# Turning the FFN's inner activations by DMA transfers of 16-bit halves in place of TensorE transposes

## The chip, the cores and the metric

The kernel runs on one core of a Trainium2 chip, as one launch. The time is device time in microseconds for one whole execution. A core has five engines with an instruction queue each: PE (TensorE: matrix products; its loads of the stationary operand are listed apart as PEld), DVE (VectorE), ACT (ScalarE), POOL (GpSimd) and SP (SyncE, which here only issues transfers). Each works through its own queue in order and waits for the others by semaphores. Transfers run on 16 DMA engines.

## The reference

One step of a one-layer backbone on 128 context and 256 latent tokens of width 2048, in float32: adaLN modulation, a mixing sub-layer (gated linear attention and a Fourier branch), and a dense SwiGLU FFN of inner width 5632. What the change touches is the FFN and the last modulation vector, `ga2`:

```python
mod = jax.nn.silu(cond) @ lw['w_ada'] + lw['b_ada']
sh1, sc1, ga1, sh2, sc2, ga2 = [m[:, None, :] for m in jnp.split(mod, N_MOD, axis=-1)]
...
h = rmsnorm(x, lw['norm_pre_ffn']) * (1.0 + sc2) + sh2
ff = (jax.nn.silu(h @ lw['w_ffn_gate']) * (h @ lw['w_ffn_up'])) @ lw['w_ffn_down']
x = x + ga2 * rmsnorm(ff, lw['norm_post_ffn'])
```

All 384 tokens go through the FFN together, as three token tiles of 128.

## The kernel before

**Numbers.** Every float32 operand of a product is split into a high part (a cast on ACT, `whi` for weights) and a low part (a subtraction on DVE, `wlo`). A product is three matmuls: high x high, low activation x high weight, high activation x low weight.

**Chunks and units.** The inner width is cut into 11 chunks of 512 (c = 0 to 10). The first runs with activations stationary the other way round and needs no turn. From c = 1 on, the table `steps` gives the order. A chunk is a row of units, each of which takes one weight tile of 128 x 1024: A0 to A3, B0 to B3, then four times C, E, D, then four times F, G, H, D. The units A, B, C, E, F, G, H make gate and up products of chunk c by a scheme that saves block products, so that some of their weight tiles are sums or differences of others, made on DVE (L1651, L1674, L1675, L1677). The D units are the down projection of chunk c - 1: D0 to D3 stand with C and E, D4 to D7 with F, G and H. On PE, A, B, C and G are 12 matmuls of 512 columns each, E, F and H six, D 18.

**Ten banks** of a chunk's products are evicted into six scratch tiles `ep` of 128 x 512 float32, called `s1`, `sq`, `s5`, `g0`, `g1`, `e2` (ep0 to ep5). At the end of the chunk `g0`, `g1` and `s5` hold the inner activations of the three token tiles, tokens on the partitions. The down projection wants them with the inner width on the partitions, so each tile is turned: in B0, B1 and B2 of the next chunk `turn_hid` issues four PE transposes of 128 x 128 into one PSUM tile `ptr` (L1812), ACT casts it to `hid_hi` and DVE subtracts to get `hid_lo` (L1814). That is done for c = 2 to 10; the chunk that comes last is turned once more, at its own place, outside of the units.

**Order.** PE, ACT, DVE and POOL run in the order in which the code is written. `grab2` is called at the start of each unit: it takes a ready weight pair, runs the list `now` on ACT, starts loads, and splits the weight tile for the unit three further on (one ACT cast, up to three entries of the list `pend`, the DVE sums, then the DVE subtraction). There are four `whi` buffers. SP's order isn't written out: a scheduler puts its transfers into one queue. Weight tiles of A and B are loaded ahead into eight resident slots; those of C, G and D go through two buffers `raw`.

**The last modulation** (`ada_last`) is a generator that is advanced by `step(ada)`. It has four quarters of 16 steps; each step loads a tile of `w_ada` of 256 KB into one of two buffers (L1704) and does two multiply-adds on DVE (L1707, L1709). A quarter ends with 16 small matmuls on PE into `pr` (L1718), an ACT copy to `adev` (L1723), a PE transpose to `ptm` (L1728) and small DVE work. These two closing parts wait, by giving up steps, while the down projection's banks are live (`d_live`). A step is taken at a rate of 0.85 per call. Whatever is left is run in one go behind unit D3 of chunk index 9.

Of the kernel before, what the change touches and what calls it, by code (L numbers as in the profile page):

```python
# [11 lines left out]
F32 = mybir.dt.float32  # L12
F32R = mybir.dt.float32r
U32 = mybir.dt.uint32
AF = mybir.ActivationFunctionType
ALU = mybir.AluOpType
PSUM = bass.MemoryType.PSUM
# [3 lines left out]
P = 128  # L21
# [13 lines left out]
FC = 4  # L35
NFC = FT // FC
G = 1024
# [70 lines left out]
def tile_step(ctx: ExitStack, tc: tile.TileContext, a, o):  # L108
    nc = tc.nc
    PE, ACT, DVE, POOL, SP = nc.tensor, nc.scalar, nc.vector, nc.gpsimd, nc.sync  # L110
# [199 lines left out]
    def take():  # L310
        return ready.pop(0)

    def grab():
        w = take()
        push()
        return w

    def step(side):
        if side is not None:
            next(side, None)  # L320
# [75 lines left out]
    def rsqrt(dst, src, scale):  # L396
        ACT.activation(dst, src, AF.Sqrt, bias=eps_t[:, 0:1], scale=scale)
        DVE.reciprocal(dst, dst)
# [10 lines left out]
    psm = ctx.enter_context(tc.tile_pool(name="psm", bufs=3, space=PSUM))  # L409
    pss = ctx.enter_context(tc.tile_pool(name="pss", bufs=5, space=PSUM))  # L410
    with ExitStack() as s:
# [94 lines left out]
        def xprod(u, kb, w, bank=px):  # L506
            def mm():
                for j, (x_, w_) in enumerate(passes(w)):
                    PE.matmul(bank, w_[:, u * P : (u + 1) * P], hT[x_][:, kb, :], start=j == 0, stop=j == 2)

            return mm, lambda dst=None: flush(xacc[u], kb == 0, dst, bank)
# [9 lines left out]

        ACT.activation(spad[:, :, 0:2], cond, AF.Silu)
        ACT.activation(tmp1, eps_t, AF.Sqrt)
        qs = [pa.tile([P, T], F32, name=f"qsA{n}") for n in range(2)]
        for k in range(KT):
            sq = qs[k] if k < 2 else scr[:, 4 + k % 4, :]
            ACT.activation(sq, xn(k), AF.Square)
            if k >= 2:
# [22 lines left out]
        for kb in range(KT):  # L551
# [59 lines left out]
            for lo, hi, c in segs:  # L611
# [4 lines left out]
                if kb == 0:  # L616
                    ACT.activation(
                        hT[0][:, kb, lo:hi], xr[:, lo:hi], AF.Identity,
                        bias=mods[:, 0, kb, c : c + 1], scale=mods[:, 1, kb, c : c + 1],
# [30 lines left out]
        for t in range(3):  # L650
            vprod(KT - 1, prev[0], range(3), (t,))
            if t < XU:
                mm, fl = xprod(t, KT - 1, prev[1])
# [99 lines left out]
    with ExitStack() as s:  # L753
# [11 lines left out]
        for c in range(2):  # L765
# [3 lines left out]
            SP.dma_start(raw3[1 + c][96:98, 0:512], src[32:33].to_broadcast([2, 512]))  # L769
        mask = pg.tile([P, 2, CH], U32, name="mask")  # L770
        ss = pg.tile([P, 3, 4], F32, name="ss")
# [7 lines left out]
        def gla():  # L779
# [10 lines left out]
            for h in range(NH):  # L790
# [26 lines left out]
                for n in range(2):  # L817
                    ACT.activation(lap[n], z[n], AF.Abs)
                ACT.activation(la, la, AF.Exp, scale=-1.0)
# [145 lines left out]
        for c in range(2):  # L965

            dst = a2.rearrange("p (h d j) -> p d h j", d=2, j=P)[:, c]
# [129 lines left out]
    with ExitStack() as s:  # L1097
# [166 lines left out]
        for b, i in mix_order:  # L1264
# [18 lines left out]
            else:  # L1283
# [10 lines left out]
                p = psm.tile([P, T], F32, tag="mm", name="pmm")  # L1294
                w = grab()
# [18 lines left out]
    with ExitStack() as s:  # L1314
# [49 lines left out]
        for i in range(KT):  # L1364
            p = psm.tile([P, T], F32, tag="mm", name="pmm")
            for g in range(2):
                n = 2 * i + g - 2 * KT
                if n < -6:
                    w = grab()
                else:  # L1370

                    w = take()
# [178 lines left out]
        def unit(t, n):  # L1551

            return psums[n // 2][:, 3 * (n % 2) + t, :]

        hid = hid_of()
# [8 lines left out]
        pend, now = [], []  # L1564

        def left_sums():

            raw = [psums[n // 3][:, 2 * (n % 3) : 2 * (n % 3) + 2, :].rearrange("p a (b c) -> p (a b) c", c=P) for n in range(4)]
            f = lambda x: x.bitcast(F32)
            h11, h12, h21, h22 = ([f(x) for x in Hx(t, k)] for t, k in ((1, 0), (1, 8), (2, 0), (2, 8)))  # L1570
            r1, r2, r4, r3 = raw
            add, sub = DVE.tensor_add, DVE.tensor_sub

            def parts(dst, src):
                return [lambda: ACT.copy(dst[0], src), lambda: sub(dst[1], src, f(dst[0]))]

            ops = [lambda: add(r1, h21[1], h22[1]), lambda: add(r1, r1, h21[0]), lambda: add(r1, r1, h22[0])]
            ops += [lambda: sub(r2, r1, h11[1]), lambda: sub(r2, r2, h11[0])]
            ops += parts(S1, r1)
            ops += [lambda: sub(r4, h12[1], r2), lambda: add(r4, r4, h12[0])]  # L1580
            ops += parts(S2, r2)
            ops += [lambda: sub(r3, h11[1], h21[1]), lambda: add(r3, r3, h11[0]), lambda: sub(r3, r3, h21[0])]
            ops += parts(S4, r4)
            return ops, parts(S3, r3)

        pend, s3_parts = left_sums()
# [100 lines left out]
        def grab2(kept=2):  # L1687
            w = take()
            while now:
                now.pop(0)()  # L1690
            load_more(kept)
            split_next()
            return w
# [52 lines left out]
        for u in range(HEAD):  # L1746
            kind, c, j = ffn_order[u]
            dst_of[kind](hp[u], c, j)
        n = 0
        for kind, c, j in ffn_order[HEAD:]:  # L1750
            p = psm.tile([P, T], F32, tag="mm", name="pmm")
# [30 lines left out]
        s1, sq, s5, g0, g1, e2 = ep  # L1782

        def evict(c, kind):
# [19 lines left out]
            elif kind == "H":  # L1804
                pend.extend([lambda: add(e2, e2, B["p4"]), lambda: mul(s5, s5, e2)])

        def turn_hid(dst, t, pool, tag):

            pt = pool.tile([P, FC, P], F32, tag=tag, name="ptr")
            src = (g0, g1, s5)[t]  # L1810
            for j in range(FC):
                PE.transpose(pt[:, j, :], src[:, j * P : (j + 1) * P], ident)  # L1812
            hi, lo = (x[:, :, t * P : (t + 1) * P] for x in dst)
            pend.extend([lambda: ACT.copy(hi, pt), lambda: DVE.tensor_sub(lo, pt, hi.bitcast(F32))])  # L1814
# [10 lines left out]
        def out(u, p, c):  # L1825
            if c == 0:
                ACT.copy(u, p)
            else:
                DVE.tensor_add(u, u, p)
            d_live[0] -= 1  # L1830
# [4 lines left out]
        for kind, c, i in steps[:-4]:  # L1835
            last_c = c == NFC - 1 and kind == "D"
            if last_c and hid_last is not None and x1b is None:
                while pend:
                    pend.pop(0)()
                x1b = actp.tile([P, KT, T], F32, tag="A_hi", name="x1b")  # L1840
                for q in range(4):
                    SP.dma_start(x1b[:, 4 * q : 4 * q + 4, :], x1_d[:, 4 * q : 4 * q + 4, :])
                ACT.activation(tmp1, eps_t, AF.Sqrt)
            if kind == "D":
                w = grab2()
                n, kh = i // 2, i % 2
                if kh == 0:
                    while pend:
                        pend.pop(0)()

                    pool, tag = (pss, "side") if done % 2 or (c, n) == (NFC - 2, 3) else (psm, "mm")
                    pd_tiles = [pool.tile([P, 512], F32, tag=tag, name="pdn") for _ in range(3)]
                    d_live[0] = 3
                h = hid_last if last_c else hid
                todo = [
                    (pd_tiles[t], [[x[:, 2 * kh + m, t * P : (t + 1) * P] for m in range(2)] for x in h], mov_d, kh == 0, kh == 1)
                    for t in range(3)
                ]
                products(w, todo)
                if kh == 1:  # L1860
                    if not last_c:
                        for t in range(3):
                            pend.append(lambda u=unit(t, n), p=pd_tiles[t], c=c: out(u, p, c))
                    else:
                        for t in range(3):
                            pend.append(lambda t=t, n=n, p=pd_tiles[t], d=done: add_last(t, n, p, d))
                        done += 1
                if not last_c and i >= 4:
                    step(ada)
                if (c, i) == (NFC - 2, 6):  # L1870

                    while pend:
                        pend.pop(0)()
                    hid_last = tuple(actp.tile([P, FC, T], F32R, tag=t, name="hidE") for t in ("C_hi", "C_lo"))
                    for t in range(3):
                        turn_hid(hid_last, t, psm, "mm")
            else:
                if kind == "A" and i == 0:
                    banks(c)
                w = grab2()  # L1880
                products(w, [(bank[c, n], two_of(stat, i), mov_gu, first and i == 0, i == 3 and last) for n, stat, first, last in of_kind[kind]])
                if i == 3:
                    evict(c, kind)
                if kind == "B" and c > 1 and i < 3:

                    turn_hid(hid, i, psm, "mm")
                if kind in "AG":
                    step(ada)
            if (kind, c, i) == ("D", NFC - 2, 3):
                while pend:  # L1890
                    pend.pop(0)()
                for _ in ada:
                    pass
# [213 lines left out]
```

## Time and profile before

| | us |
|---|---|
| median of 3 runs (lowest, highest) | 1935.93 (1934.81, 1936.08) |
| the profiled execution's own time | 1935.18 |
| its span in the trace | 1933.4 |
| PE busy in the span | 1916.9 |
| DVE busy | 1652.2 |
| ACT busy | 915.8 |
| one FFN chunk, from B0's transposes to the next chunk's | 93.94 or 94.94 |

The page is one profiled execution on the core. Its busy times are shares of the span; a matmul's end is modelled, and matmuls overlap, so PE's cost is better read from the distances between starts. A stretch of the trace gives busy time per engine between two moments, and the order of time gives start, duration, engine, line, tile and, in brackets, the idle time ahead and what ended it. In the FFN the granted clock of PE is 1.00 throughout.

### The profile page before, as it was taken

The numbers are of one execution on the slowest core, as the hardware profiler recorded it, in microseconds if no ns is written. First come the engines' busy times: TensorE is split into PE (matmuls) and PEld (weight loads), VectorE is DVE, ScalarE is ACT, GpSimd is POOL, SyncE is SP. The second block draws the span as 40 slices with busy tenths as digits, with TensorE's granted clock in tenths as the row PEclk, the third lists the DMA queues.
The fourth block names the chain that finished last, engine by engine and source line by source line (L and its number), as shares of the span: only waits on it lengthen the run. The fifth ranks groups of instructions, "written<-read, shape, count | busy, mean of one in ns | idle before, by whom it ended". The sixth has DMA issues, their size and how long they took to land.

```text
span 1933.4 us, 27462 instructions
## 1 busy us (share of the span) xinstructions
PE 1916.9 (99%) x10494; PEld 1689.6 (87%) x10494; DVE 1652.2 (85%) x2172; ACT 915.8 (47%) x1298; POOL 82.7 (4%) x146
## 2 busy tenths in 40 slices
PE   8999999999999999999999999999999999999998
PEld 5679999999999999999988888888888888888886
DVE  5659897989968898978789888998998999887876
ACT  4235455545446654456455444444444444444445
POOL 0001111100000000104000000000000000000000
PEclk9999999999999999999999999999999999999999
DMA  9976766766657886665264636363636373626244
GB/s 389 391 277 233 257 227 228 262 216 208 219 174 245 294 289 205 234 208 198 80 190 139 198 102 194 116 213 100 211 113 209 92 222 93 213 66 196 70 153 149
DMA packets 200904, 380.53 MB, mean 197 GB/s; under 512 B 14228, under 2 KB 126964, under 8 KB 196420
## 3 DMA queue, kind: packets, MB, share of 16 engines
q1 hardware_dynamic: 181540, 320.84, 49.5%
q0 software_dynamic: 13952, 50.39, 8.8%
q10 hardware_dynamic: 5280, 7.55, 1.1%
q8 instruction: 82, 1.34, 0.3%
q14 instruction: 50, 0.41, 0.1%
HBM read 361.94 MB, written 16.78 MB: 196 GB/s over the span
## 4 chain that ended last, share of the span: by engine, by line
PE 93%; DVE 3%; DMA 3%; ACT 1%; issue 1%; SPq 0%; DVEq 0%; ACTq 0%
PE pmm L326 31%; PE pgu L338 31%; PE pdn L338 18%; PE pv L491 3%; DMA slab<-in_w_ada 2%; PE pfo L1043 1%; PE pgm L474 1%; PE pf L1243 1%; PE pmm L1520 1%; PE ptr L1812 1%; PE pfo L1044 1%; PE pf L1244 1%; PE po L788 1%; DVE wlo L287 0%; DMA raw<-in_w_d 0%
## 5 line engine op out<-in xcount | busy, mean ns | idle before, releaser
L326 PE MATMUL pmm<-A_hi,whi 128*128 128x384 f32 x1088 | 366.8, 337 | 0.0
L326 PE MATMUL pmm<-A_lo,whi 128*128 128x384 f32 x1088 | 364.1, 335 | 0.3 <-DVE A_lo L379 0.3
L326 PE MATMUL pmm<-A_hi,wlo 128*128 128x384 f32 x1088 | 364.1, 335 | 0.0
L1667 ACT CAST whi<-u 128x1024 fp32r<-128x1024 f32 x200 | 210.6, 1053 | 272.5 <-DVE u L1651 86.2
L1667 ACT CAST whi<-raw 128x1024 fp32r<-128x1024 f32 x175 | 184.2, 1053 | 211.9 <-PE pgu L338 66.1
L1678 DVE TENSOR_TENSOR wlo<-u,whi 128x1024 fp32r<-128x1024 f32 x200 | 244.1, 1221 | 27.1 <-ACT whi L1667 16.3
L338 PE MATMUL pgu<-whi,A_hi 128*128 128x512 f32 x640 | 250.0, 391 | 0.0
L338 PE MATMUL pgu<-whi,A_lo 128*128 128x512 f32 x640 | 249.3, 389 | 0.0
L1678 DVE TENSOR_TENSOR wlo<-raw,whi 128x1024 fp32r<-128x1024 f32 x175 | 213.4, 1220 | 34.4 <-ACT whi L1667 25.1
L287 DVE TENSOR_TENSOR wlo<-raw,whi 128x1024 fp32r<-128x1024 f32 x165 | 200.7, 1220 | 30.6 <-ACT whi L300 30.2
L300 ACT CAST whi<-raw 128x1024 fp32r<-128x1024 f32 x151 | 158.1, 1050 | 118.8 <-PE pmm L326 43.1
L707 DVE SCALAR_TENSOR_TENSOR adacc<-adaw,spad,adacc 128x1024 f32<-128x1024 f32 x170 | 210.5, 1280 | 1.5 <-DMA adaw<-in_w_ada 1.2
L326 PEld LDWEIGHTS pmm<-A_hi,whi 128*128 128x128 f32 x1088 | 204.2, 188 | 3.3 <-issue 2.5
L326 PEld LDWEIGHTS pmm<-A_lo,whi 128*128 128x128 f32 x1088 | 204.4, 188 | 1.0 <-DVE A_lo L379 0.8
L326 PEld LDWEIGHTS pmm<-A_hi,wlo 128*128 128x128 f32 x1088 | 204.2, 188 | 0.3 <-DVE wlo L287 0.2
L338 PE MATMUL pdn<-whi,hid_hi 128*128 128x512 f32 x480 | 186.9, 389 | 0.0
L338 PE MATMUL pdn<-whi,hid_lo 128*128 128x512 f32 x480 | 186.8, 389 | 0.0
L338 PE MATMUL pgu<-wlo,A_hi 128*128 128x512 f32 x640 | 184.2, 389 | 0.0
L338 PEld LDWEIGHTS pgu<-whi,A_hi 128*128 128x128 f32 x640 | 120.2, 188 | 26.1 <-issue 0.8
L338 PEld LDWEIGHTS pgu<-wlo,A_hi 128*128 128x128 f32 x640 | 120.1, 188 | 25.4
L338 PEld LDWEIGHTS pgu<-whi,A_lo 128*128 128x128 f32 x640 | 120.1, 188 | 25.0
L338 PE MATMUL pgu<-whi,S 128*128 128x512 f32 x480 | 131.1, 395 | 0.0
(400 smaller groups left out, 2998.3 us busy)
## 6 DMA issues: line engine op xcount, KB each, us to landing
adaw<-in_w_ada POOLq DMA_DIRECT2D x96, 512.0 KB, 4.0
raw<-in_w_d SPq DMA_DIRECT2D x88, 512.0 KB, 3.9
slab<-in_w_ada SPq DMA_DIRECT2D x32, 1024.0 KB, 10.6
raw<-in_w_gate SPq DMA_DIRECT2D x64, 512.0 KB, 4.4
raw<-in_w_g SPq DMA_DIRECT2D x48, 512.0 KB, 3.8
raw<-in_w_u SPq DMA_DIRECT2D x48, 512.0 KB, 3.8
raw<-in_w_in SPq DMA_DIRECT2D x46, 512.0 KB, 4.3
u<-in_w_u SPq DMA_DIRECT2D x40, 512.0 KB, 4.7
```

What stands on the lines that cost most here:

```text
L287: eng.tensor_sub(lo, raw, hi.bitcast(F32))
L300: ACT.copy(hi, raw)
L326: PE.matmul(dst, w[wi][:, k * n + n0 : k * n + n0 + P], x[xi][:, k0 + k, :], start=first and k == 0 and j == 0, stop=last and k == kts - 1 ...
L338: PE.matmul(dst, stat[x_][m], mov(w[w_], m), start=first and w_ == m == x_ == 0, stop=last and w_ == m == 1,)
L474: PE.matmul(pgv[q : q + 32, :], spad[:, k, :], slab[k // (KT // 2)][:, k % (KT // 2), :], start=k < 4, stop=k >= KT - 4,)
L491: PE.matmul(pv[2 * t + g], hT[x_][:, kb, t * P : (t + 1) * P], w_[:, g * 512 : (g + 1) * 512], start=kb == 0 and j == 0, stop=kb == KT - 1 ...
L707: DVE.scalar_tensor_tensor(acc[:, c, :], w, spad[:, k, c : c + 1], acc[:, c, :], op0=ALU.mult, op1=ALU.add,)
L788: PE.matmul(dst, w[wi], x[xi], start=first and j == 0, stop=last and j == 2)
L1043: PE.matmul(p, w_of[0][:, i, k, g, :], x[:, :, lo:hi], start=kt == 0, stop=False)
L1044: PE.matmul(p[:, 0], w_of[1][:, i, k, g, :], x[:, 0, lo:hi], start=False, stop=kt == KT - 1)
L1667: ACT.copy(hi, src)
L1678: DVE.tensor_sub(lo, src, hi.bitcast(F32))
```

## The change

The PE transposes of c = 2 to 10 go. In their place stand two halves. `send_hid` at A0, A2 and B1: ACT copies the tile's 512 float32 per partition, seen as 1024 16-bit numbers, into a spare `ep` tile so that the first halves of all numbers stand together and the second halves behind them; SP then issues one transfer that transposes the 128 x 1024 16-bit numbers in eight blocks of 128 x 128 into another spare tile. `take_hid` at A3, B0 and B3: ACT copies the turned halves together again into a third spare tile, casts that to `hid_hi`, and leaves the subtraction for `hid_lo` to DVE. The turn of the last chunk stays on PE.

The steps of the last modulation are taken away from the A units and given to D0 to D3; at D4 to D7 and at G they stay. That is four calls for four per chunk.

```diff
+        planes_in, turned_in, whole_in = (sq, s1, g0), (e2, g1, s5), (g0, e2, g1)
+
+        def as_u16(x):
+            return x.bitcast(U16).rearrange("p (x h) -> p h x", h=2)
+
+        def send_hid(t):
+
+            planes = planes_in[t].bitcast(U16)
+            ACT.copy(planes.rearrange("p (h x) -> p h x", h=2), as_u16((g0, g1, s5)[t]))
+            SP.dma_start(turned_in[t].bitcast(U16).rearrange("p (b x) -> p b x", x=P), planes, transpose=True)
+
+        def take_hid(dst, t):
+
+            hi, lo = (x[:, :, t * P : (t + 1) * P] for x in dst)
+            ACT.copy(as_u16(whole_in[t]), turned_in[t].bitcast(U16).rearrange("p (h x) -> p h x", h=2))
+            w = whole_in[t].rearrange("p (j x) -> p j x", j=FC)
+            ACT.copy(hi, w)
+            pend.append(lambda: DVE.tensor_sub(lo, w, hi.bitcast(F32)))
+
+        turning = {
+            ("A", 0): (send_hid, 0), ("A", 2): (send_hid, 1), ("A", 3): (take_hid, 0),
+            ("B", 0): (take_hid, 1), ("B", 1): (send_hid, 2), ("B", 3): (take_hid, 2),
+        }
...
-                if not last_c and i >= 4:
+                if not last_c:
                     step(ada)
...
-                if kind == "B" and c > 1 and i < 3:
-
-                    turn_hid(hid, i, psm, "mm")
-                if kind in "AG":
+                if c > 1 and (kind, i) in turning:
+                    what, t = turning[kind, i]
+                    what(*(() if what is send_hid else (hid,)), t)
+                if kind == "G":
                     step(ada)
```

How the instructions stand now is seen at three places. First ACT in chunk 4, units A0 to B2, before: `pgu` are the banks of unit A, `ptr` the transposed tiles.

```order
L1667 CAST whi_11783<-u012_9280 128x1024
L1667 CAST whi_11803<-u012_9280 128x1024
L1667 CAST whi_11823<-u012_9280 128x1024
L1790 COPY ep0_7646<-pgu_11750 128x512
L1790 COPY ep1_7647<-pgu_11751 128x512
L1667 CAST whi_11845<-u345_9281 128x1024
L1667 CAST whi_11866<-raw_11645 128x1024
L1814 CAST hid_hi_9285<-ptr_11861 128x4x128
```

The same place in the change:

```order
L1816 COPY ep1_7647<-ep3_7649 128x1024
L1668 CAST whi_11752<-u012_9280 128x1024
L1668 CAST whi_11769<-u012_9280 128x1024
L1816 COPY ep0_7646<-ep4_7650 128x1024
L1668 CAST whi_11788<-u012_9280 128x1024
L1822 COPY ep3_7649<-ep5_7651 128x2x512
L1824 CAST hid_hi_9285<-ep3_7649 128x4x128
L1791 COPY ep0_7646<-pgu_11720 128x512
L1791 COPY ep1_7647<-pgu_11721 128x512
L1668 CAST whi_11809<-u345_9281 128x1024
L1822 COPY ep5_7651<-ep4_7650 128x2x512
L1824 CAST hid_hi_9285<-ep5_7651 128x4x128
```

L1816 is a send's copy, L1822 and L1824 a take. The evictions of A's banks overwrite `s1` (ep0) and `sq` (ep1), from which the second and the first transfer read, so they now stand behind those transfers, and the cast for B3 (`u345`, the row after them) behind the evictions.

Second, SP at the same chunk, before and in the change:

```order
L1637 DMA raw_11685<-in_w_d 128x2x512
L1704 DMA w5_9683<-in_w_ada 128x512 x6
L1637 DMA raw_11891<-in_w_g 128x4x256
L1637 DMA raw_11935<-in_w_d 128x2x512
L1637 DMA raw_11955<-in_w_g 128x4x256
```

```order
L1638 DMA raw_11655<-in_w_d 128x2x512
L1705 DMA w5_9899<-in_w_ada 128x512
L1817 DMA_TRANSPOSE ep5_7651<-ep1_7647 128x8x128
L1705 DMA w5_9899<-in_w_ada 128x512
L1817 DMA_TRANSPOSE ep4_7650<-ep0_7646 128x8x128
L1817 DMA_TRANSPOSE ep2_7648<-ep3_7649 128x8x128
L1638 DMA raw_11849<-in_w_g 128x4x256
```

The three transposing transfers stand ahead of the load for C1 (`raw<-in_w_g` after them); of the modulation's loads at this place two remain.

Third, PE where the last quarter of the modulation is closed, in the change, behind unit D3 of chunk index 9:

```order
L339 MATMUL pdn_16256<-wlo_16251,hid_hi_9285 128x512 x2
L1719 MATMUL pr_16337<-acc5_9898,selr_87 32x128 x8
L1729 MATMUL ptm_16348<-ident_74,adev_16346 128x128
L339 MATMUL pgu_15943<-whi_16277,A_hi_8983 128x512
L339 MATMUL pgu_15943<-whi_16277,A_lo_8984 128x512
```

Before, and for the other three quarters in the change too, a unit or more of products stands between `pr` and `ptm`; here they follow each other, with ACT's copy to `adev` between them.

More of the change, by code (lines that the diff above doesn't have):

```diff
@@ L14 @@
 U32 = mybir.dt.uint32
+U16 = mybir.dt.uint16
 AF = mybir.ActivationFunctionType
```

## The prediction

> **What bounds the kernel now.** I read the page's busy time and chain first, then the stretches from one turn of the inner activations to the next, then the order of time inside one of them. The page says:
>
> ```profile
> span 1933.4 us, 27462 instructions
> PE 1916.9 (99%) x10494; PEld 1689.6 (87%) x10494; DVE 1652.2 (85%) x2172; ACT 915.8 (47%) x1298; POOL 82.7 (4%) x146
> PE 93%; DVE 3%; DMA 3%; ACT 1%; issue 1%; SPq 0%; DVEq 0%; ACTq 0%
> ```
>
> Busy PE alone could hide gaps, since matmul ends are modelled. So I cut the FFN at the transposes, which return once per chunk, and take busy time by stretch (us, busy PE, PEld, DVE, ACT, POOL, clock, DMA share, GB/s):
>
> ```profile
> 1143.50:1237.44 93.94, 93.94 (x422) 77.75 (x420) 85.13 (x95) 38.99 (x42) 0.00 (x0) 1.00 0.51 160
> 1237.44:1332.38 94.94, 94.94 (x439) 78.13 (x437) 88.39 (x100) 44.21 (x49) 0.00 (x0) 1.00 0.50 155
> 1710.14:1804.08 93.94, 93.94 (x422) 77.75 (x420) 77.22 (x80) 42.73 (x46) 0.00 (x0) 1.00 0.44 135
> ```
>
> The chunk lasts 93.94 us whether DVE is busy for 85 us or for 77 us; 94.94 us stands where the modulation's closing matmuls fall in. A period that doesn't move with the load of DVE or ACT is PE's own: what leaves PE leaves the time, as long as nothing else becomes late.
>
> **What the transposes cost on PE.** The order of time on PE in chunk 2 (start, us, count):
>
> ```profile
> 1048.56 0.60 PE L1812 MATMUL ptr<-ident,ep 128*128 128x128 f32 x4
> ...
> 1058.17 0.39 PE L338 MATMUL pgu<-whi,A_hi 128*128 128x512 f32 x1
> ...
> 1062.26 0.39 PE L338 MATMUL pdn<-whi,hid_hi 128*128 128x512 f32 x1
> ...
> 1066.34 0.39 PE L338 MATMUL pgu<-whi,A_hi 128*128 128x512 f32 x1
> ```
>
> A D unit is 18 matmuls in 1066.34 - 1062.26 = 4.08 us, 0.2267 us each. From the first transposes to 1058.17 stand 36 such matmuls and 12 transposes: 9.61 - 36 x 0.2267 = 1.45 us for the 12. As a check, a chunk has 8 x 12 + 4 x 36 + 4 x 42 = 408 matmuls: 408 x 0.2267 = 92.5, and 93.94 - 92.5 = 1.45. Nine chunks (c = 2 to 10) lose them: **9 x 1.45 = -13.1 us**. The twelve transposes of the last chunk stay.
>
> **What PE gets in return.** In the changed order the last quarter of the modulation is closed behind unit D 9,3 with `pr` and its transpose `ptm` back to back. Where the first quarter is closed in before, the order of time has:
>
> ```profile
> 1131.71 0.65 PE L1718 MATMUL pr<-acc,selr 128*32 128x128 f32 x16
> 1132.28 0.50 PE L338 MATMUL pgu<-whi,A_hi 128*128 128x512 f32 x1
> 1132.42 0.27 ACT L1723 COPY adev<-pr 128x128 f32<-128x128 f32 x1 [3.58 <-PE pr L1718]
> ```
>
> PE could go on at 1132.28 and the copy ends at 1132.69, so PE will wait at least 0.4 us once; at most one cast more (1.05 us) if ACT comes late, 1.5. I take **+0.5 us**, since here ACT had waited 3.58 us for PE.
>
> **What ACT and DVE get.** Per tile ACT gets two copies of 1024 elements a lane; its casts of that size are the nearest rows:
>
> ```profile
> L1667 ACT CAST whi<-u 128x1024 fp32r<-128x1024 f32 x200 | 210.6, 1053 | 272.5 <-DVE u L1651 86.2
> 1223.84:1247.05 23.21, 23.21 (x109) 19.19 (x108) 23.18 (x28) 7.31 (x9) 0.00 (x0) 1.00 0.19 57
> 1247.05:1279.70 32.65, 32.65 (x146) 27.04 (x145) 30.58 (x32) 16.55 (x20) 0.00 (x0) 1.00 0.50 150
> 1153.00:1186.00 33.00, 33.00 (x148) 27.31 (x147) 26.40 (x27) 14.64 (x16) 0.00 (x0) 1.00 0.45 137
> 1219.78 23.95 SPq L1704 DMA_DIRECT2D w<-in_w_ada  x6
> ```
>
> That is 27 x 2 x 1.05 = 57 us, all in units A and B, the first stretch: 7.31 + 6 x 1.05 = 13.6 of then 21.8 us. It fits; below nothing it can't be, and if 16-bit elements took twice as long, 19.9 us would still fit, barely. DVE has the opposite: it is full in A and B (23.18 of 23.21) and the change takes the modulation's four steps out of there. They go to units C to D3, the second stretch, whose 30.58 holds work left over from the first; one chunk earlier it had 26.40, and with four steps at the rate 0.85 and 1.41 us each it comes to 31.2 of 33, still under PE. Each step takes its load along: SP had six of them in one row, spread over 23.95 us by their waits for DVE; now one at most stands among the sends, with its buffer long free, and holds none up. **Zero** for both engines in the sum, covered by PE; the cover ends where ACT is made to wait for a transfer.
>
> **The transfers' place on the path.** No transfer that transposes is in the trace of before. The rows nearest to it:
>
> ```profile
> w<-in_w_ada SPq DMA_DIRECT2D x64, 256.0 KB, 2.7
> out_yT<-x1b SPq DMA_DIRECT2D x11, 256.0 KB, 2.5
> slab<-in_w_ada SPq DMA_DIRECT2D x32, 1024.0 KB, 10.6
> ```
>
> Each new transfer is 256 KB (128 x 1024 of two bytes), so L, issue to landing, is hardly under 2.5 us. From above: its rows are 1024 runs of 256 bytes. Over 930 to 1900 us the queue of SP shows
>
> ```profile
> q1 hardware_dynamic: 113497, 144.87, 48.0%
> ```
>
> 970 us x 16 engines x 0.48 / 113497 = 66 ns per packet; with one packet per run, 1024 / 16 x 66 ns = 4.2 us, and 1.8 us around it (2.7 less some 0.9 of moving at that packet rate) make 6.0. I take 4, in the middle, since bytes and queue are those of the 2.7 us row and only the runs are shorter. Eight 128 x 128 blocks one after another would be worse; that is a rival.
>
> What L may be follows from chunk 4 of the trace, where unit A0 begins on PE at 1223.84:
>
> ```profile
> L1814 ACT CAST hid_hi<-ptr x27: 569/581/592, 1050.9 to 1811.1; 128x512 fp32r<-128x512 f32 x27
> L1814 DVE TENSOR_TENSOR hid_lo<-ptr,hid_hi x27: 678/684/693, 1052.4 to 1811.7; 128x512 fp32r<-128x512 f32 x27
> ...
> 1222.72 1.06 ACT L1667 CAST whi<-u 128x1024 fp32r<-128x1024 f32 x1 [2.12 <-PE pdn L338]
> 1230.24 1.06 ACT L1667 CAST whi<-u 128x1024 fp32r<-128x1024 f32 x1 [6.46 <-DVE u L1651]
> 1238.38 1.07 ACT L1790 COPY ep<-pgu 128x512 f32<-128x512 f32 x2
> ...
> 1224.04 0.69 DVE L1805 TENSOR_TENSOR ep<-ep,ep 128x512 f32<-128x512 f32 x1
> 1228.91 1.22 DVE L1651 TENSOR_TENSOR u<-u,u 128x1024 f32<-128x1024 f32 x1
> 1231.18 1.41 DVE L1709 SCALAR_TENSOR_TENSOR acc<-w,spad,acc 128x512 f32<-128x512 f32 x2
> ...
> 1248.58 0.38 SPq L1637 DMA_DIRECT2D raw<-in_w_g  x1
> ...
> 1251.13 0.39 PE L338 MATMUL pdn<-whi,hid_hi 128*128 128x512 f32 x1
> ```
>
> The cast behind A0 ends at 1223.8, `e2` is free at 1224.7, so the first transfer starts at 1224.9 and has until take 0, about 1235.8: 10 us. Without the step at 1231.18 the sums follow each other by 2.27 us, so the casts for B1 and B2 end at 1233.5 and 1235.8; the second send stands between them and its transfer starts at 1234.6. Take 0 ends at 1237.4. Behind it in ACT's order stand the copies of banks p1 and q1 into `s1` and `sq`; the second transfer reads `s1`, so they wait for its landing, at 1234.6 + L. Those copies (1.07), the cast for B3 (1.05), take 1 (1.05 + 0.58), the cast for C0 (1.05) and the third send's copy (1.05) follow each other: 5.8 us. The third transfer starts at 1240.4 + L (L over 2.8), lands at 1240.4 + 2L, and take 2 (1.05 + 0.58) and DVE's part (0.68) end at 1242.7 + 2L. PE needs that tile at D0's ninth matmul: 1251.13 - 1.45 + 8 x 0.2267 = 1251.5. So nothing is late up to **L = 4.4**; at 4 there is 0.8 us to spare. The cast for B3 (1236.7 + L against 1242.9) is the looser bound. SP is not the tight place: the next weight load left at 1248.58 in before, and the third transfer is issued ahead of it. Beyond 4.4 a chunk loses 2(L - 4.4) at first, but PE's wait lets DVE make up its lag (the cast at 1230.24 stood 6.46 us for DVE and could have run about 3.5 us sooner), so it settles at L - 4.4 until 3.5 us are used up, then 2L - 12.3. This holds in eight chunks; ahead of the last one the modulation's steps run out, and with them the lag.
>
> In a sentence by itself: the Trainium skill, DMA: Bandwidth & Descriptors, section "Latency and other measured facts", gives 261 GB/s for a transposing transfer with a non-contiguous middle dimension; by it moving would take an estimated 1.0 us, L would be near 3, and the sum would stay as it is. No run here shows it yet.
>
> **Sum.** 1935.18 us is the profiled execution's own time (span 1933.4 and 1.8 around it): 1935.2 - 13.1 + 0.5 = 1922.6. The median of the runs shown, 1935.93, is 0.75 above it, so for the median I say **1923.4 us**.
>
> **Rivals.** *Partly eaten:* L between 4.4 and 6. At L = 6.0, my upper bound, eight chunks lose 1.6 us each, 12.8, and nothing is left: 1936. For it speaks that the margin at L = 4 is below 1 us; against it, that the 6.0 counts each run as a packet of its own with the mean packet's time, though the mean packet has 1276 bytes.
>
> *The transfers are slow:* from L = 6 on the kernel is slower than before. The place is the third transfer, behind ACT's copies that wait for the second. If its blocks go one after another, the slowest landing of the page's larger groups, 10.6 us, is a price: 2 x 10.6 - 12.3 = 8.9 us a chunk, with all nine 80, so 1923.4 + 80 = 2003. Against it speaks that 256 KB took 2.7 us from the same queue; for it, that no row shows a transfer that turns its data. Beside it stands a rule: the Trainium skill, VectorE: DVE Perf Modes, section "The three transpose paths", has 1309 ns for one 128 x 128 block of 16-bit elements by DMA; eight in series are an estimated 10.5 us, and by that rule it is this rival. It hasn't been seen here.
>
> *DVE becomes the bound:* 88.39 us of busy time against then 92.5 us of PE leaves 4 us, so only with waits on top. In-order waits for the casts of the turned tiles could do it; a loss of 1.5 us a chunk would give 1936. I count it to "no change".
>
> *The change doesn't do what it says,* two-byte pieces being moved singly: 131072 / 16 x 66 ns = 540 us a transfer, some 14 ms more. The built program has one transposing instruction per tile, so I give it under 0.02.
>
> **Chances.** All hidden (1921.5 to 1927) 0.55; partly eaten but still faster 0.12; no change 0.08; slower 0.25, of which half beyond 1975. A difference of 0.2%, 3.9 us, is about what a measurement of this kernel can tell from none: faster 0.67, same 0.08, slower 0.25. The range goes from 1921.5 (all 13.1 and no wait at `ptm`, with the runs' spread) to 1975, L near 9, and leaves out some 0.15. The likeliest case's own range is 1921.5 to 1927.
>
> **What would show it.** Right: the stretches between the same units last 92.5 us; PE doesn't wait for `hid_hi` or `hid_lo` at D0; the transposing transfers land within 4.4 us; A and B on ACT hold about 13.6 us of work. Wrong: a landing over 6 us, ACT standing at the copies of p1 and q1 behind a transfer, PE's idle time ahead of the first `pdn` matmuls. Most easily wrong is L, then the DVE lag that sets where the sends begin.

## The result and the profile after

The changed kernel takes 1924.68 us (median of 4 runs, 1924.01 to 1925.97) against 1936.01 us (4 runs, 1934.81 to 1937.04): the ratio is 0.9946, 95% interval 0.9933 to 0.9958, so 11.3 us less. Its profiled execution took 1925.33 us. From its page, busy time and the chain's shares:

```profile
span 1923.5 us, 27404 instructions
PE 1903.9 (99%) x10386; PEld 1678.5 (87%) x10386; DVE 1651.7 (86%) x2172; ACT 974.6 (51%) x1352; POOL 82.4 (4%) x146
PE 92%; DVE 3%; DMA 3%; ACT 1%; issue 1%; SPq 0%; DVEq 0%; ACTq 0%
```

PE has 108 instructions and 13.0 us less, ACT 58.8 us more, DVE the same. PE still sets the end. The stretches from one unit D0 to the next (us, busy PE, PEld, DVE, ACT, POOL, clock, DMA share, GB/s), then one chunk's units A and B, then its C to D3:

```profile
1061.48:1153.96 92.48, 92.48 (x410) 76.58 (x408) 85.27 (x93) 49.48 (x52) 0.00 (x0) 1.00 0.54 163
1153.96:1247.44 93.48, 93.48 (x427) 76.94 (x425) 78.48 (x87) 47.55 (x51) 0.00 (x0) 1.00 0.48 147
1247.44:1339.92 92.48, 92.48 (x410) 76.58 (x408) 89.49 (x100) 48.88 (x52) 0.00 (x0) 1.00 0.57 174
...
1221.60:1243.36 21.76, 21.76 (x98) 18.02 (x96) 20.01 (x22) 14.57 (x16) 0.00 (x0) 1.00 0.20 46
1243.36:1276.00 32.64, 32.64 (x146) 27.03 (x144) 31.69 (x35) 15.64 (x16) 0.00 (x0) 1.00 0.57 171
```

A chunk lasts 92.48 us where it lasted 93.94 (1.0 more where `pr` falls in, as before), and PE doesn't wait in it, though DVE is busy for 89.49 us of one chunk.

To see where the whole difference sits, I took the stretch from the first D0 of the FFN (c = 1) to that of c = 10 and the rest behind it, of before:

```profile
968.32:1817.77 849.45, 849.45 (x3849) 701.30 (x3848) 767.59 (x837) 389.79 (x424) 0.00 (x0) 1.00 0.49 153
1817.77:1933.30 115.53, 107.67 (x507) 89.35 (x505) 84.52 (x133) 53.65 (x84) 3.42 (x8) 0.99 0.45 146
```

and of after:

```profile
969.00:1804.37 835.37, 835.37 (x3724) 690.24 (x3723) 764.60 (x835) 446.41 (x474) 0.00 (x0) 1.00 0.54 164
1804.37:1923.40 119.03, 108.86 (x524) 89.68 (x522) 87.64 (x138) 54.78 (x86) 3.40 (x8) 0.98 0.44 142
```

The nine chunks give 14.1 us back; 1.0 of it is one closing `pr`, which has moved behind them. The rest of the kernel has 3.5 us more. 2.1 of these stand at that closing (`pdn` are the banks of the down projection):

```profile
1831.57 1.52 PE L339 MATMUL pdn<-wlo,hid_hi 128*128 128x512 f32 x6
1833.90 0.64 PE L1719 MATMUL pr<-acc,selr 128*32 128x128 f32 x16 [0.81 <-DVE psums L1854]
1834.93 0.33 PE L1729 MATMUL ptm<-ident,adev 128*128 128x128 f32 x1 [0.39 <-ACT adev L1724]
1835.02 0.48 PE L339 MATMUL pgu<-whi,A_hi 128*128 128x512 f32 x1
```

The six matmuls of D3 take 6 x 0.2267 = 1.36 us, to 1832.93; from there to 1835.02 are 2.09 us, against 1.0 us where the closing falls into a chunk. Of the remaining 1.4 us, 1.0 lie between the last turn and the kernel's last down projections, where PE waits for DVE's half of the last turned tile (`hidE`): 35.25 us in before, 36.25 here and 35.60 in a second profile of the same kernel. As the two profiles of one kernel differ by 0.65 us there, the runs don't tell how much of it is the change's own.

The new instructions of the turns, by line (duration ns min/median/max; the last row is the transfers' time from issue to landing):

```profile
L1816 ACT COPY ep<-ep x27: 1035/1038/1070, 1036.9 to 1796.0; 128x1024 uint16<-128x1024 uint16 x27
...
L1822 ACT COPY ep<-ep x27: 1347/1366/1376, 1045.7 to 1800.3; 128x1024 uint16<-128x1024 uint16 x27
...
L1824 ACT CAST hid_hi<-ep x27: 619/621/627, 1047.1 to 1801.7; 128x512 fp32r<-128x512 f32 x27
...
L1825 DVE TENSOR_TENSOR hid_lo<-ep,hid_hi x27: 676/691/694, 1048.0 to 1802.4; 128x512 fp32r<-128x512 f32 x27
...
L1817 SPq DMA_TRANSPOSE ep<-ep x27: 1232/1232/1362, 1038.0 to 1797.1; - x27
...
DMA to landing us min/median/max: 3.0/3.0/3.2
```

A turning transfer lands 3.0 us after its issue. In chunk 4 the third tile passes through ACT, DVE and PE like this (order of time):

```profile
1235.41 1.07 ACT L1791 COPY ep<-pgu 128x512 f32<-128x512 f32 x2
...
1240.19 1.04 ACT L1816 COPY ep<-ep 128x1024 uint16<-128x1024 uint16 x1
...
1244.31 1.36 ACT L1822 COPY ep<-ep 128x1024 uint16<-128x1024 uint16 x1 [1.02 <-DMA ep<-ep]
...
1246.36 0.69 DVE L1825 TENSOR_TENSOR hid_lo<-ep,hid_hi 128x512 fp32r<-128x512 f32 x1 [0.62 <-ACT hid_hi L1824]
...
1249.48 0.39 PE L339 MATMUL pdn<-whi,hid_lo 128*128 128x512 f32 x1
```

`hid_lo` is done at 1247.05 and PE reads it at 1249.48: **2.4 us of room**. ACT waits 1.02 us for the transfer, which costs nothing. The copies of banks p1 and q1, at 1235.41, don't wait for the second transfer.

### The profile page after: what moved, and what is told of

The parts are those of the page before. It is cut to its first block, busy times and chain, and to the rows that moved or that the text cites. A ratio compares the mean times of both kernels' runs of the same rounds, so it can differ in the third digit from the quotient of the medians.

```text
span 1923.5 us, 27404 instructions
## 1 busy us (share of the span) xinstructions
PE 1903.9 (99%) x10386; PEld 1678.5 (87%) x10386; DVE 1651.7 (86%) x2172; ACT 974.6 (51%) x1352; POOL 82.4 (4%) x146
## 3 DMA queue, kind: packets, MB, share of 16 engines
q1 hardware_dynamic: 210052, 327.92, 51.5%
## 4 chain that ended last, share of the span: by engine, by line
PE 92%; DVE 3%; DMA 3%; ACT 1%; issue 1%; SPq 0%; DVEq 0%; ACTq 0%
PE pmm L327 31%; PE pgu L339 31%; PE pdn L339 18%; PE pv L492 3%; DMA slab<-in_w_ada 2%; PE pfo L1044 1%; PE pf L1244 1%; PE pgm L475 1%; PE pmm L1521 1%; PE pfo L1045 1%; PE pf L1245 1%; PE po L789 1%; DVE wlo L288 1%; DMA raw<-in_w_d 0%; DMA raw<-in_w_v 0%
## 5 line engine op out<-in xcount | busy, mean ns | idle before, releaser
L1679 DVE TENSOR_TENSOR wlo<-raw,whi 128x1024 fp32r<-128x1024 f32 x175 | 213.1, 1218 | 22.7 <-PE pdn L339 11.8
```

What stands on the lines that cost most here:

```text
L1679: DVE.tensor_sub(lo, src, hi.bitcast(F32))
```

## The experiments

My theory: the transposes' 1.45 us a chunk are the whole gain, and it stays whole because each transfer lands within its room; a later transfer eats it. The rivals: the gain comes from the moved modulation steps; DVE's and ACT's slack absorbs a late transfer; or the blocks of a transfer are moved one after another. All edits are against the changed kernel.

**The transfers alone.**

```diff
-                if not last_c:
+                if not last_c and i >= 4:
                     step(ada)
...
-                if kind == "G":
+                if kind in "AG":
                     step(ada)
```

> The transfers stay, and the last modulation's steps go back to units A, G and D4 to D7. Theory (room): the steps had to leave A and B, because there DVE is full. With them back the casts for B1 to B3 follow each other by about 3.6 us and not 2.27, the sends and takes on ACT slide behind them, and the third tile is ready about 1 us after PE wants it at D0, in some seven chunks; the burst of 1.1 us behind unit D3 of chunk index 9 goes away: 1927 to 1933 us. Rival (only PE counts): where the steps stand makes no difference, 13 us are gained by the transposes that left PE, 1923 to 1924 us.

Measured: 1926.77 us (1926.37 to 1927.67), ratio 0.9957 (0.9942 to 0.9972). The nine chunks as one stretch:

```profile
968.83:1809.20 840.37, 837.84 (x3741) 690.36 (x3740) 766.01 (x836) 451.01 (x478) 0.00 (x0) 1.00 0.55 163
```

PE's only wait of any size in the FFN's table of waits (us in total, times, longest):

```profile
PE pgu L339 <- DVE wlo L1679: 2.5, 3, 1.0
```

and one of the three in the order of time:

```profile
1246.77 0.72 PE L339 MATMUL pgu<-wlo,A_hi 128*128 128x512 f32 x2 [1.00 <-DVE wlo L1679]
```

Without waits these would be 836.4 us, all four closings being inside; 4.0 are lost, at three places (the table counts 2.5 of them as idle; the matmuls' overlapping ends hide the rest), and 1.1 come back since the closing's burst is gone. What is late is not the third tile but `wlo` of C0: DVE, with the steps still in A, runs the sums of A and B 3.6 us apart instead of 2.27, and the weight pairs behind them come late. So the transfers bring the gain, and the moved steps keep some 3 us of it by the traces; by the medians it is 1 to 2, with intervals that overlap.

**The steps alone.** PE's transposes are put back, the steps stay where the change has them:

```diff
-                if c > 1 and (kind, i) in turning:
-                    what, t = turning[kind, i]
-                    what(*(() if what is send_hid else (hid,)), t)
+                if kind == "B" and c > 1 and i < 3:
+                    turn_hid(hid, i, psm, "mm")
```

> The transposes are back on PE in B0 to B2, and the modulation's steps stay at D0 to D7 and G. Theory (PE sets the chunk): no gain, the chunk is 93.9 us again, and the burst is paid: 1936 to 1938 us. Rival (DVE's relief in A and B is part of the gain): below 1934 us.

Measured: 1936.74 us (1936.06 to 1938.16), ratio 1.0008 (0.9998 to 1.0017). The nine chunks:

```profile
968.28:1816.73 848.45, 848.45 (x3833) 700.93 (x3831) 769.87 (x837) 389.36 (x421) 0.00 (x0) 1.00 0.48 153
```

That is before's 849.45 less the one closing that moved out. The steps' move is worth nothing by itself; the first rival falls.

**Each transfer twice.** The second one writes the same data to the same place, so takers wait for two:

```diff
             SP.dma_start(turned_in[t].bitcast(U16).rearrange("p (b x) -> p b x", x=P), planes, transpose=True)
+            SP.dma_start(turned_in[t].bitcast(U16).rearrange("p (b x) -> p b x", x=P), planes, transpose=True)
```

> As the change, but each tile's transfer is issued twice into the same place, the second one waiting for the first, so that issue to landing is 6.0 to 6.3 us in place of the 3.0 us measured in the change. Theory (the landing may take up to about 4.1 us: at D0 the third tile was 2.2 us early in the change, and each further us counts twice there, once through the second transfer and once through the third): each of nine chunks loses about 2 us, 1938 to 1948 us. Rival (the transfers have ample room): 1924 to 1926 us, chunk 92.5 us.

Measured: 1978.68 us, ratio 1.0224 (1.0207 to 1.0241), dearer than either expected. PE's waits:

```profile
PE pdn L339 <- ACT hid_hi L1825: 21.1, 8, 3.2
PE pgu L339 <- DVE wlo L1679: 6.0, 7, 1.1
```

One of the first kind, at D0's ninth matmul, in the order of time:

```profile
1264.62 0.50 PE L339 MATMUL pdn<-whi,hid_hi 128*128 128x512 f32 x1 [2.62 <-ACT hid_hi L1825]
```

The stretches of the nine chunks together, of this wait, of the ten matmuls behind it, and of what comes next:

```profile
969.49:1855.93 886.44, 855.01 (x3724) 696.27 (x3723) 761.54 (x832) 440.77 (x469) 0.00 (x0) 0.99 0.55 162
...
1261.61:1264.62 3.01, 0.39 (x2) 0.00 (x1) 0.02 (x1) 2.00 (x3) 0.00 (x0) 1.00 0.60 186
1264.62:1269.10 4.48, 4.26 (x11) 3.15 (x11) 4.48 (x5) 3.37 (x4) 0.00 (x0) 0.62 0.00 0
1269.10:1273.00 3.90, 3.90 (x19) 3.21 (x18) 3.74 (x5) 0.49 (x1) 0.00 (x0) 1.00 0.61 170
```

The third tile is late, as the theory has it. In chunk 4 ACT goes on 6.2 us after the second tile's first issue (1243.30 to 1249.50) and 7.2 us after the third's (1255.37 to 1262.59), so the third landed later than expected. Of the 51.1 us lost, 31.4 are idle PE and 19.6 are more busy time. Part of that is a lower clock: behind the wait of 2.62 us the granted clock is 0.62 for 4.48 us, in which PE does ten matmuls that take 10 x 0.2267 = 2.27 us at 1.00 and waits 0.22 us once more. The trace has seven such stretches of 3.41 us at 0.50, so they cost at most 7 x 1.7 = 11.9 us; part of the rest is the 0.16 us by which a matmul's busy time reaches into each wait (0.39 us long, 0.2267 to the next start). My expectation had only the waiting in it.

**Eight transfers of one block each** in place of one of eight blocks:

```diff
-            SP.dma_start(turned_in[t].bitcast(U16).rearrange("p (b x) -> p b x", x=P), planes, transpose=True)
+            turned = turned_in[t].bitcast(U16)
+            for b in range(8):
+                SP.dma_start(turned[:, b * P : (b + 1) * P], planes[:, b * P : (b + 1) * P], transpose=True)
```

> As the change, but each tile's transfer is issued as eight transfers of one 128 x 128 block each. In the change one transfer of eight blocks holds SP for 1.23 us and lands after 3.0 us. Theory (the time is per block, 0.15 us of issue each): last landing 3 to 4.2 us after the first issue, 1924 to 1927 us. Rival (the time is per transfer, about 1.2 us of issue each): last landing after 10 to 12 us, some 10 us lost in each of nine chunks, 2000 to 2040 us.

Measured: 2087.76 us, ratio 1.0788 (1.0767 to 1.081). The eight issues of one tile in SP's order of time:

```profile
1039.01 10.13 SPq L1819 DMA_TRANSPOSE ep<-ep  x8
```

All issues of the line:

```profile
L1819 SPq DMA_TRANSPOSE ep<-ep x216: 1094/1230/2352, 1039.0 to 1961.8; - x108
...
DMA to landing us min/median/max: 2.2/2.4/4.3
```

The nine chunks:

```profile
970.01:1958.18 988.17, 882.19 (x3725) 717.65 (x3723) 763.18 (x832) 442.96 (x469) 0.00 (x0) 0.93 0.45 138
```

SP is held 1.23 us by one block as by eight. A single block lands 2.4 us after its issue in the median (2.2 at least), eight in one transfer after 3.0, so the blocks of a transfer are not moved one after another at a single block's price. 152.8 us are lost in the chunks: 106.0 idle, 46.8 in longer busy time, most of it at half clock (mean clock 0.93).

**Plain transfers ahead of each send**, one and three, of the same 256 KB to HBM (here with one; with three, the range is 3):

```diff
+            for n in range(1):
+                SP.dma_start(spare_d[n], planes)
             SP.dma_start(turned_in[t].bitcast(U16).rearrange("p (b x) -> p b x", x=P), planes, transpose=True)
```

> As the change, with one plain store of the same 256 KB to HBM issued ahead of each transposing transfer, which makes the transfer land some 0.4 to 0.7 us later after its send. Theory (2.2 us of room at D0, each us of landing counts twice there): 2 x 0.7 is less than 2.2, no loss, 1924 to 1926 us, chunk 92.5 us. Rival (the chain is already at its limit): 0.5 to 1.4 us a chunk, 1929 to 1937 us.

> As before it, with three stores ahead of each transfer, which should delay the landing by 1.2 to 2 us. Theory (room 2.2 us, each us counts twice): 2 x 1.2 to 2 x 2 less 2.2 is 0.2 to 1.8 us a chunk, with nine chunks 2 to 16 us: 1926 to 1941 us. Rival (each us counts once, room 2.2 us): no loss, 1924 to 1926 us.

Measured: 1928.3 us (1925.97 to 1929.74), ratio 0.9963 (0.9948 to 0.9978), with one; 1948.3 (1947.1 to 1949.51), ratio 1.0068 (1.005 to 1.0087), with three. Both lose more than the theory gave. The nine chunks with one store take 839.69 us, 4.3 over the change's, which is 0.5 us a chunk, the lower end of what the rival had; PE's waits there begin with

```profile
PE pgu L339 <- DVE wlo L1679: 1.7, 3, 1.0
```

With three they take 857.15 us, 21.8 over, of which 12.7 us are idle PE. ACT at the two transfers that it waits for in chunk 4, in the order of time:

```profile
1241.15 1.08 ACT L1791 COPY ep<-pgu 128x512 f32<-128x512 f32 x2 [3.65 <-DMA ep<-ep]
...
1252.01 1.35 ACT L1825 COPY ep<-ep 128x1024 uint16<-128x1024 uint16 x1 [2.99 <-DMA ep<-ep]
```

The first thing to become late is again C0's `wlo`, and the way there is the eviction of p1 and q1: it overwrites what the second transfer reads, ACT stands at it, B3's cast stands behind it, and DVE stands in its own queue at that cast. In the change this eviction came just in time. The third tile was delayed as expected: its take in chunk 4 begins 3.5 us after the send's copy with one store and 5.0 with three, against 3.1 in the change. The second transfer was delayed more than that: in chunk 4 it landed 4.9 and 5.4 us after its issue, against 3.0 in the change and a median of 3.1 and 3.5 over the landings on record in these two kernels. The store ahead of it reads the same tile and could hold the eviction too, but the stores landed after 2.0 to 3.1 us, before it. Why the second transfer was so late there is not shown.

**The third send one unit later**, to try the 2.4 us directly:

```diff
-            ("B", 0): (take_hid, 1), ("B", 1): (send_hid, 2), ("B", 3): (take_hid, 2),
+            ("B", 0): (take_hid, 1), ("B", 2): (send_hid, 2), ("B", 3): (take_hid, 2),
```

> The third tile's send (ACT copy and transfer) one unit later, at B2 in place of B1; nothing else. In the change, chunk 4, the send's copy ended at 1241.23, the copy that takes the tile began at 1244.31 (after 1.02 us of waiting for the transfer), the third hid_lo was done at 1247.05 and PE read it at 1249.48: 2.4 us of room. Behind the cast that ended at 1243.30 the send's copy ends at about 1244.3, so everything up to hid_lo comes 3.0 us later, 1250.1, 0.6 us too late; C0's sums and subtractions stand behind hid_lo on DVE and come 2.1 us late where they begin at 1249.3. Theory (the room at the third tile is 2.4 us as the trace shows): PE waits 0.5 to 1.5 us a chunk in nine chunks, 1929 to 1938 us, and the waits ended by hid_hi, hid_lo or wlo of C0 on PE's rows. Rival 1 (the room is larger, since ACT and DVE catch up by the slack they have in front of B0): 1924 to 1926. Rival 2 (loss of the whole 3.0 us): over 1945.

Measured: 1934.36 us (1933.62 to 1939.09, 11 runs), ratio 1.0002 (0.9993 to 1.0011): the whole gain is gone by one unit of delay, at 1.05 us a chunk in the mean (nine chunks take 844.78 us, 9.4 over the change's), as the theory said. In chunk 4 ACT's send and take and DVE's `hid_lo` in the order of time:

```profile
1242.36 1.04 ACT L1816 COPY ep<-ep 128x1024 uint16<-128x1024 uint16 x1
...
1246.54 1.35 ACT L1822 COPY ep<-ep 128x1024 uint16<-128x1024 uint16 x1 [2.19 <-DMA ep<-ep]
...
1248.57 0.69 DVE L1825 TENSOR_TENSOR hid_lo<-ep,hid_hi 128x512 fp32r<-128x512 f32 x1 [2.71 <-ACT hid_hi L1824]
```

The copy starts 2.17 us later, not 3.0, since it went ahead of a cast that I had put before it; `hid_lo` is done at 1249.26 and read at 1249.60. Here the room just held; in other chunks it didn't. In the dearest, c = 7, the tile took 4.4 us from the end of the send's copy to the take (1527.93 to 1532.33; in chunk 4, 3.1). Its stretches (D0's first eight matmuls, the wait, then its last ten in two pieces):

```profile
1530.59:1532.40 1.81, 1.81 (x9) 1.31 (x7) 0.00 (x0) 0.07 (x1) 0.00 (x0) 1.00 0.69 161
1532.40:1534.36 1.96, 0.16 (x1) 0.00 (x1) 0.02 (x1) 1.93 (x3) 0.00 (x0) 1.00 1.03 359
1534.36:1536.24 1.88, 1.66 (x5) 1.11 (x6) 1.88 (x3) 1.38 (x2) 0.00 (x0) 0.79 0.26 99
1536.24:1538.80 2.56, 2.56 (x8) 1.99 (x7) 2.56 (x3) 1.99 (x2) 0.00 (x0) 0.50 0.00 0
```

A wait of 1.8 us made D0 4.1 us longer (8.21 against 4.08): the clock fell to 0.50 behind it. That is 4.1 of the 9.4 us, so the loss is uneven: from the first D0 to the fourth the three chunks take 278.44 us, as in the change.

**The last closing one unit earlier**, to save the burst's 1.1 us:

```diff
-                if kind == "G":
+                if kind == "G" or (kind == "A" and c == NFC - 1):
                     step(ada)
```

> As the change, but in the last chunk (c = 10) the modulation's generator is also advanced at A0 to A3, so that the last quarter's pr and ptm stand two units apart and not back to back behind unit D3 of chunk index 9. Theory (the burst is a real cost): in the change PE stood 0.97 us for pr's bank and 0.39 us for adev there; these go, and the program gains about 1.1 us over the change: 1923 to 1924.5 us, PE without a wait at ptm. Rival (it is hidden or comes back at the end): as the change, 1924.7 us, within 0.3.

Measured: 1924.98 us (1924.01 to 1926.28, 5 runs), ratio 0.9947 (0.9933 to 0.9961). The waits at `pr` and `ptm` are gone, but the transposes of the last turn, which did not wait in the change, now wait 1.3 us:

```profile
PE ptr L1837 <- DVE ep L1806: 0.7, 1, 0.7
PE ptr L1837 <- DVE ep L1803: 0.6, 1, 0.6
```

No gain that can be told from the change: DVE's chain in front of the last turn is next in line.

**The change again**, on one chip with the kernels with stores and with the earlier closing:

> The change itself once more, on the same chip as its variants: 1924 to 1926 us, 0.9946 of before or within 0.001 of that.

Measured: 1925.69 us (1924.52 to 1926.51, 5 runs), before 1935.04 (10 runs), ratio 0.9951 (0.9938 to 0.9963); the nine chunks took 836.05 us and PE waited 0.8 and 0.4 us at the closing, as in the first profile. No kernel here beats the change by more than the runs differ.

## Why the prediction came out right, and where its steps were wrong

1923.4 us was predicted; 1924.68 and 1925.69 were measured, inside the likeliest case's own range. As a gain, 12.5 us was predicted (from 1935.93), and 11.3 and 9.4 were measured against the runs of before beside them. The nine chunks gave 13.1 us in the first profile and 12.4 in the second (849.45 - 836.05, less the one closing), of 13.1 forecast; the rest of the miss lies behind them, at the closing and in the stretch behind the last turn, and in what the runs differ by.

- **PE is the bound, and what leaves PE leaves the time: right.** 93.94 - 92.48 = 1.46 us a chunk, predicted 1.45; nine chunks give 13.1.
- **The burst at the last closing, +0.5: the term was too small.** It costs 1.1. I had only ACT's copy in mind, and that wait is the 0.39 us I named. The 0.81 us before it are a wait of `pr` for its bank, which the first of DVE's three additions of D3's results (680 ns each) still holds. The row I took as a model stood between other units, where no such additions are due. The sum with 1.1 is 1924.0.
- **L = 4: too high, harmlessly.** It is 3.0. The upper bound of 6 took the mean packet's 66 ns. In after the queue has 210052 packets at 51.5% of a span of 1923.5 us, in before, over its whole span, 49.5% of 1933.4, with 28511 packets fewer in all: (1923.5 x 0.515 - 1933.4 x 0.495) x 16 / 28511 = an estimated 19 ns for a packet more. The shorter packets of these transfers took less time than the mean one, which I noted against that bound and should have used.
- **ACT's copies at 1.05 us each: one right, one not.** 1.04 for the send, 1.37 for the take, which writes with a stride. A and B on ACT hold 14.57 us of 21.76, predicted 13.6 of 21.8: covered, as said. DVE's second stretch: 31.69 of 32.64, predicted 31.2 of 33.
- **The moved steps at zero: right for the change** (the steps alone change nothing), but they are a condition, not a free extra: without the move the transfers lose 4.0 us in the chunks.
- **The room: right at the place I looked at, and not the only bound.** "Nothing is late up to L = 4.4" left 2.8 us at L = 3.0; the trace shows 2.4 (the take's copy, 1.37 us in place of 1.05, makes 0.3 of the difference), and the third send's move agrees with it. But the looser bound that I set aside, B3's cast behind the second transfer, is the one that gave way first in the kernels with stores, through C0's `wlo`.
- **What a late transfer costs, L - 4.4 a chunk: wrong.** Two things failed. PE's wait does not let DVE make up its lag: DVE stands in its own queue for the turned tile (in the kernel with doubled transfers it waited 51.4 us for `hid_hi`, and B0's cast still stood 5.5 us behind DVE). And a wait of PE costs more than its length, as the half clock behind it shows. For eight pieces, L is 7 x 1.25 + 2.4 = 11.2 us; the rival's formula 2L - 12.3 gives 10.1 us a chunk, the idle time is 106.0 / 9 = 11.8, and 46.8 / 9 = 5.2 come on top. So the rival "the transfers are slow" was priced at some 40% too little. The range's upper end of 1975, which stood for L near 9, was passed much earlier: with the doubled transfers, at 6.2 and 7.2 us in chunk 4, the time was 1978.7, and a chunk lost 51.1 / 9 = 5.7 us where L - 4.4 gives 1.8 to 2.8. The prediction holds because L came out at 3.0; its account of a late transfer was not needed.
- **The rule by which eight blocks are an estimated 10.5 us** (the Trainium skill, VectorE: DVE Perf Modes, section "The three transpose paths") does not hold for blocks in one transfer: 3.0 us measured, while a single block alone took 2.4 us from issue to landing. The estimate of L near 3 from the Trainium skill, DMA: Bandwidth & Descriptors, section "Latency and other measured facts", agrees with the trace.

## What to carry to other kernels

Where PE is busy without a gap, count what leaves its queue by the spacing of its matmuls; here that gave the chunks' gain to within 0.1 us in the first profile and 0.7 in the second, and everything else in the change only had to stay hidden. For a transfer put in the place of PE work, work out for each buffer it reads and writes who waits next on which in-order queue: the tight place was not only the consumer of the data but also the overwriting of its source. And where a wait of PE comes near 2 us, reckon with up to 1.7 us on top of it, for a stretch of 3.41 us at half clock.

## What the runs showed of the hardware that I had not expected

- **The clock after a wait.** In the chunks of all these kernels every wait of PE of up to 1.36 us left the granted clock at 1.00; of twelve waits from 1.77 to 3.21 us, nine were followed by 3.41 us at 0.50 and three (2.09, 2.56 and 2.70) by none; all eighteen of 5.28 us and more, in the kernel with eight pieces, brought the clock down while they lasted. The Trainium skill, TensorE: Matmul & The Clock Gate, section "Part 1: The HAM clock gate", says that the clock falls to half after an idle window of about 3.4 us, and that the windows run freely. The traces agree with free-running windows: in the kernel with doubled transfers the seven stretches at 0.50 last 3.41 us each and begin at 1067.45, 1166.43, 1265.42, 1364.41, 1565.79, 1664.78 and 1763.77, which is 29, 29, 29, 59, 29 and 29 times 3.413 us apart. But a window need not be idle from end to end. Two waits of like length in that kernel, cut by the same grid into windows:

```profile
1262.01:1265.42 3.41, 0.58 (x2) 0.26 (x2) 0.82 (x2) 2.80 (x4) 0.00 (x0) 1.00 0.39 137
1265.42:1268.83 3.41, 3.41 (x8) 2.70 (x9) 3.41 (x4) 2.57 (x3) 0.00 (x0) 0.50 0.00 0
...
1459.98:1463.39 3.41, 1.85 (x9) 1.19 (x7) 0.00 (x0) 1.02 (x1) 0.00 (x0) 1.00 1.07 284
1463.39:1466.80 3.41, 2.18 (x8) 1.61 (x9) 2.42 (x3) 2.86 (x5) 0.00 (x0) 1.00 0.02 5
```

The wait of 2.62 us lies in one window, in which PE is idle for 2.8 us, and the next window has 0.50. The wait of 2.56 us falls on two windows, with 1.6 and 1.2 us idle, and the clock stays. In the chunks of all kernels, windows at full clock with 1.90 us idle or more were followed by half clock and those with up to 1.56 us were not; in between, one with 1.72 was and one with 1.88 wasn't. So here about half a window sufficed, and whether a wait near 2 us costs more than itself depends on where it falls.

- **The issue of a transposing transfer** holds SP for 1.23 us, with one block as with eight; a plain load's issue takes 0.35 to 0.38 us on the same queue in the change.
- **ACT's 16-bit copies**: 1.04 us where the read is strided, 1.37 where the write is, for the same 128 x 1024.
